# A decoder trunk for a prompt and eight samples: weight splits on VectorE, padded score rows, an earlier load, and output rows in two pieces

## The chip, the cores and the metric

The kernel runs on one core of a Trainium2 chip. The metric is the device time of one execution in microseconds (us); the time of a kernel is the median over its runs. Engines are named as the profile names them: PE is TensorE, DVE is VectorE, ACT is ScalarE, POOL is GpSimd, SP is SyncE, which issues most of the DMAs.

## The reference

The reference is one step of a two-layer decoder trunk. It runs for a prompt of 512 tokens and for eight samples of four new tokens each (32 in all), with the same weights and a width of 1024. In outline:

```python
def trunk(x, pos, pool_prev, ckv_past, krope_past, mem_k, mem_v, ...):
    # layer A
    z = rmsnorm(x, g_norm[0]) @ w_in_a[0]
    u, gate_t, q_m, gate_m = split(z)              # 1024, 1024, 512, 512
    tok = pool_mix(concat(prev, u), ...)           # trailing means of 2, 4, 8, 16, minus self, times w_pool_grp
    x = x + concat(tok * silu(gate_t), mem_attend(q_m) * silu(gate_m)) @ w_out[0]
    # the shared key/value side
    ckv, krope = shared_latent_kv(x, ...)          # 256 and 64 wide
    # layer B
    z = rmsnorm(x, g_norm[1]) @ w_in_b[0]
    c_q, gate_t, q_m, gate_m = split(z)            # 384, 1024, 512, 512
    tok = mla_mix(c_q, pos, concat(ckv_past, ckv), concat(krope_past, krope), ...)
    x = x + concat(tok * silu(gate_t), mem_attend(q_m) * silu(gate_m)) @ w_out[1]
    return rmsnorm(x, g_final), ...
```

In `mla_mix` eight heads attend over the latent: scores are `q_lat . ckv + q_rope . krope`, values are `p . ckv`, taken through `w_v_up` afterwards. The prompt attends to its own 512 positions. A sample attends to 4096 cached positions, which lie in 32 pages of 128 named by a page table, and to its own new rows. The outputs are the normalized streams of prompt and samples and the new states (pooling rows, latents, keys and values of the memory).

## The kernel before, in words

**Layout and precision.** Prompt and sample columns lie side by side, 544 columns, worked on in two halves of 272. Activations are transposed, so features are on the 128 partitions. Every large product is made of three matmuls: `split` (L88) casts an operand to its high part on ScalarE (L89) and subtracts it from the operand to get the low part (L90), on VectorE or on the engine that it is given; `mm3` (L93 to L96) then multiplies high by high (L94), high by low (L95) and low by high (L96) into one PSUM bank.

**Layer A.** The weights `w_in_a` come in slabs of 128 output features, a tile of 128x1024. `weights` (L234) loads a slab on SP into `wr` (three buffers) and splits it into `wh` and `wl` (two buffers each in the pool `pw`, and one more in `pw2`); without an engine given, GpSimd computes the low part. The memory attention comes first, then the pooling stage. In that stage ten slabs (the list `stage`: eight for the pooling branch's input, two for gates) are loaded and split ahead by `prepare_a` (L546), each two units before it is used. `pool_unit` (L571) makes one slab of the branch: the product, its evacuation by VectorE (L578, L581), then the running sums, also on VectorE: `g + 1` additions over 678 columns (L604), a correction of 16 columns (L606), the mean minus self for the prompt (L608) and for the samples (L611), and the split of the result. A gate's product is evacuated by VectorE too (L251, one per half), and its SiLU takes ScalarE and VectorE (L264, L265). `pool_mixed` multiplies two such slabs by a group's matrix and evacuates the product with the gate (L634). Four PSUM banks, `pa`, serve all these products, so TensorE goes on only when VectorE has emptied one.

**Layer B.** Behind the latent (`ckT_s` and `krT_s` keep its 32 new columns apart for the samples) stands a stage whose order is written by hand for PE and SP: generators yield estimates of their time, and `weave` (L956) always takes the one that is most behind. Their instructions stand in the program in that order. The threads are:

- the rounds over the samples' pages: `load_half` (L996) loads tiles `a` and `b` through SP; scores (L1051, L1062), transposes (L135), values (L1090)
- the prompt's heads
- `own_scores` (L1432), once: for each of eight samples, the scores of its 32 head-and-row queries against its four new rows, two matmuls over 128 rows of the latent (L1438) and one over the 64 rotary rows (L1441)
- `out_all`, the prompt's output projection: `out_rows(fh)` (L1379) for each half of the 1024 output columns. Six slabs of `w_out_b` (two 128-row blocks by 512 columns) are loaded into `wr` by `slab` (L1349) and split with GpSimd by `prepare`; for each slab the four row blocks of 128 tokens, in the order 0, 3, 1, 2, accumulate into four `oa` banks. `done` adds the residual (L1392) and squares and sums on ScalarE (L1393). For the second half it also adds the two halves' sums (L1398), takes the reciprocal root (L155 on VectorE, L159 on GpSimd), scales the first half on ScalarE (L1402) and the second half with the gain on VectorE (L1404), and stores both (L1403, L1405).
- `sample_out` (L1581), the samples' output: it issues the loads of five `w_out_b` slabs into `ws` (five buffers), then the load of `o`, the parts of all samples' attention that were stored in DRAM (`ostore`, L1585), then two tiles `vx` of `w_v_up` (L1590). `combine` joins the parts with the new rows' part (L1532), transposes, copies (L1549), and multiplies by `w_v_up` (L1561). Then twelve slabs are multiplied by 32 columns (L1598), a new slab's load going out as each buffer is read; the result is added to the residual (L1610), and behind both halves the samples are normalized (L1618).

VectorE, ScalarE and GpSimd are ordered by a scheduler that runs while the program is built, with estimates of its own. So an edit in one place can move instructions of these engines elsewhere.

Of the kernel before, what the change touches and what calls it, by code (L numbers as in the profile page):

```python
# [38 lines left out]
def trunk_kernel(ctx: ExitStack, tc: tile.TileContext, A, O):  # L39
# [506 lines left out]
    def prepare_a():  # L546
        if stage:
            f = stage.pop(0)
            ahead_a.append(weights(wa, f, pw2 if len(stage) % 3 == 1 else None))

# [236 lines left out]
    ckT_s = cst([P, 2, NS])  # L787
    krT_s = cst([64, NS])
    for f in range(2):
        nc.vector.tensor_copy(ckT_s[:, f, :], ck[f][:, SEQ:])  # L790
    nc.vector.tensor_copy(krT_s, kr[:64, SEQ:])
    ckx = [split(pc("c", F32R), pc("c", F32R), ck[f][:, :SEQ]) for f in range(2)]
# [546 lines left out]
    wo = A["w_out_b"]  # L1339
    ssq = st(8)  # L1340
    sss = st(2)
# [37 lines left out]
    def out_rows(fh):  # L1379
        pts = [ps_("oa") for _ in range(4)]  # L1380
        pts = [pts[j] for j in (0, 3, 1, 2)]

        def run(s, j, wh, wl):
            c = slice(j * P, (j + 1) * P)
            for i, k in enumerate(order[s]):
                h, l = mixed[k]
                mm3(pts[j], h[:, c], l[:, c], wh[:, i, :], wl[:, i, :], s == 0 and i == 0, s == 5 and i == 1)

        def done(j):
            f = slice(fh * 512, (fh + 1) * 512)  # L1390
            xf = x1n[j][:, f]
            nc.vector.tensor_tensor(out=xf, in0=pts[j], in1=xf, op=ALU.add)  # L1392
# [11 lines left out]
            nc.vector.scalar_tensor_tensor(out=xf, in0=xf, scalar=r, in1=gains_f[0][:, f], op0=ALU.mult, op1=ALU.mult)  # L1404
            nc.sync.dma_start(O["y_p"][0, j * P : (j + 1) * P, 512:], xf)  # L1405

        late = []
        for s in range(6):
# [4 lines left out]
            for j in range(4):  # L1413
                for one in late:
                    run(one[0], j, *one[1:])
                    yield 1.4, 0.0
                if s == 5:
                    if not x1n:
                        yield lambda: x1n
                    done(j)  # L1420
            for _ in late:
# [10 lines left out]
    def own_scores():  # L1432
# [3 lines left out]
        for b in range(NB):  # L1436
            for k in range(2):
# [3 lines left out]
            nc.tensor.matmul(  # L1441
                sv[:, b, :], lhsT=Qr[:64, b, 0, :], rhs=krT_s[:, b * NT : (b + 1) * NT], start=False, stop=True
            )
# [314 lines left out]
```

## Time and profile before

| | us |
|---|---|
| median of three runs | 838.99 |
| lowest and highest of them | 835.16, 840.82 |
| the profiled execution, its own time | 837.61 |
| its span in the profile | 835.8 |
| TensorE busy with matmuls | 793.3 |
| VectorE, ScalarE, GpSimd busy | 502.9, 326.7, 261.0 |

The page shows one execution. A row of a timeline has the start in us from the beginning of the span, the duration in us, the engine, the line, the operation, the tile written and the tile read, the shapes, and how many alike were merged (x4). In brackets stands how long the engine had been idle before it and what ended that idle time. A window's row gives busy time and count for each engine, then the granted TensorE clock (1.00 is full), the DMA share and GB/s. In the chain of waits each piece is released by the one before it, so its shares add up to the whole span. SPq is the queue of SP: the time it spends in issuing DMAs.

### The profile page before, as it was taken

What the parts mean: (1) busy time and instruction counts of PE and PEld (TensorE: products, weight loads), DVE (VectorE), ACT (ScalarE), POOL (GpSimd) and SP (SyncE); (2) the same over time, 40 slices, a digit from 0 to 9 for tenths busy, and PEclk for the clock granted to TensorE, in tenths of its full rate; (3) what the DMA queues carried; (4) which work ended last, traced back from release to release, by engine and by line L of the source; (5) the groups of instructions that cost most, each with busy time, mean ns of one, the idle gap of its engine ahead of it and who ended that gap; (6) DMA issues with size and microseconds to landing.
All of it is one profiled execution on the core that took longest, in us unless ns stands there. A gap on an engine that the chain in (4) does not pass through costs nothing.

```text
span 835.8 us, 17542 instructions
## 1 busy us (share of the span) xinstructions
PE 793.3 (95%) x6906; PEld 681.5 (82%) x6906; DVE 502.9 (60%) x941; ACT 326.7 (39%) x650; POOL 261.0 (31%) x213
## 2 busy tenths in 40 slices
PE   6999999988999999999999999899999999999995
PEld 6989998988999989877999897676767767767674
DVE  6757666797763435775766653665665577653313
ACT  7453343322243226335433423444443445342212
POOL 0035224444133313411522242642250230055321
PEclk9999999998999999999999999999999999999998
DMA  8355247421213234636624785967978767886652
GB/s 305 97 185 219 74 176 253 158 76 45 96 57 96 75 121 149 204 91 223 227 88 179 264 282 194 367 220 238 307 243 269 260 217 243 269 274 221 219 177 107
DMA packets 82101, 158.01 MB, mean 189 GB/s; under 512 B 9186, under 2 KB 34403, under 8 KB 81763
## 3 DMA queue, kind: packets, MB, share of 16 engines
q1 hardware_dynamic: 77170, 141.22, 50.7%
q0 software_dynamic: 4848, 15.67, 5.1%
q8 instruction: 54, 0.88, 0.4%
q14 instruction: 29, 0.23, 0.1%
HBM read 147.23 MB, written 9.64 MB: 188 GB/s over the span
## 4 chain that ended last, share of the span: by engine, by line
PE 72%; DVE 12%; DMA 8%; issue 2%; ACT 2%; POOL 2%; SPq 1%; POOLq 0%; DVEq 0%; ACTq 0%
PE pa L94 14%; PE pa L96 13%; PE pa L95 13%; PE tr L135 5%; PE ac L1051 3%; PE ac L1090 3%; DVE v L604 3%; DMA o<-ostore 2%; PE oa L94 2%; PE oa L95 2%; PE oa L96 2%; PE ac L1062 2%; PE ac L393 1%; DMA b<-in_cache_P 1%; DMA wr<-in_w_mem_v 1%
## 5 line engine op out<-in xcount | busy, mean ns | idle before, releaser
L94 PE MATMUL pa<-h,wh 128*128 128x272 f32 x832 | 240.2, 291 | 0.9 <-DVE g L634 0.9
L96 PE MATMUL pa<-h,wl 128*128 128x272 f32 x832 | 236.9, 290 | 0.7 <-POOL wl L90 0.7
L90 POOL TENSOR_TENSOR wl<-wr,wh 128x1024 fp32r<-128x1024 f32 (+1 forms) x67 | 154.8, 2311 | 232.3 <-ACT wh L89 220.9
L95 PE MATMUL pa<-h,wh 128*128 128x272 f32 x640 | 184.4, 289 | 0.0
L94 PEld LDWEIGHTS pa<-h,wh 128*128 128x128 f32 x832 | 157.1, 189 | 5.6 <-issue 3.5
L96 PEld LDWEIGHTS pa<-h,wl 128*128 128x128 f32 x832 | 155.7, 189 | 2.2 <-POOL wl L90 1.2
L89 ACT CAST wh<-wr 128x1024 fp32r<-128x1024 f32 (+1 forms) x87 | 87.7, 1008 | 173.2 <-PE pa L95 69.0
L95 PEld LDWEIGHTS pa<-h,wh 128*128 128x128 f32 x640 | 121.1, 189 | 1.0
L95 PE MATMUL pa<-g,wh 128*128 128x272 f32 x192 | 54.9, 289 | 0.5 <-DVE g L90 0.5
L265 DVE SCALAR_TENSOR_TENSOR g<-t,g 128x272 f32<-128x272 f32 x48 | 46.1, 968 | 13.9 <-ACT t L264 13.9
L264 ACT ACTIVATE t<-g 128x272 f32<-128x272 f32 x48 | 20.3, 429 | 82.2 <-DVE g L251 77.7
L135 PE MATMUL tr<-c,b 128*128 128x128 f32 x256 | 39.6, 277 | 3.0 <-DVE kt L1019 1.7
L94 PE MATMUL oa<-wh,c 128*128 128x512 f32 x96 | 39.5, 412 | 0.0
L95 PE MATMUL oa<-wl,c 128*128 128x512 f32 x96 | 38.0, 396 | 1.2 <-POOL wl L90 1.2
L135 PEld LDWEIGHTS tr<-c,b 128*128 128x128 f32 x256 | 29.6, 140 | 9.5 <-issue 3.0
L95 PEld LDWEIGHTS pa<-g,wh 128*128 128x128 f32 x192 | 36.2, 188 | 0.9 <-DVE g L90 0.9
L1017 ACT COPY kt<-tr 128x512 f32<-128x512 f32 x43 | 25.3, 589 | 26.3 <-PE tr L135 25.4
L1051 PE MATMUL ac<-kt,c 128*32 128x256 f32 x256 | 34.4, 386 | 0.0
L1051 PE MATMUL ac<-a,c 128*32 128x256 f32 x256 | 34.0, 386 | 0.0
L251 DVE SCALAR_TENSOR_TENSOR g<-pa,r 128x272 f32<-128x272 f32 x42 | 18.1, 437 | 25.8 <-PE pa L96 25.7
L90 DVE TENSOR_TENSOR q<-q,q 128x512 fp32r<-128x512 f32 x16 | 27.2, 1698 | 10.0 <-ACT q L89 9.9
L90 DVE TENSOR_TENSOR wl<-wr,wh 128x1024 fp32r<-128x1024 f32 x20 | 24.5, 1225 | 12.4 <-ACT wh L89 12.3
(380 smaller groups left out, 1813.9 us busy)
## 6 DMA issues: line engine op xcount, KB each, us to landing
a<-in_cache_P SPq DMA_DIRECT2D x128, 288.0 KB, 4.7
b<-in_cache_P SPq DMA_DIRECT2D x128, 160.0 KB, 4.9
wr<-in_w_in_a SPq DMA_DIRECT2D x24, 512.0 KB, 3.8
wr<-in_w_in_b SPq DMA_DIRECT2D x19, 512.0 KB, 3.6
cs<-in_mem_kT SPq DMA_DIRECT2D x16, 512.0 KB, 5.4
wr<-in_w_out_a SPq DMA_DIRECT2D x16, 384.0 KB, 3.1
wr<-in_w_out_b SPq DMA_DIRECT2D x12, 512.0 KB, 5.6
ws<-in_w_out_b SPq DMA_DIRECT2D x12, 512.0 KB, 5.5
```

The lines of the kernel that those rows point to most:

```text
L89: nc.scalar.copy(h, src)
L90: (eng or nc.vector).tensor_tensor(out=l, in0=src, in1=fr(h), op=ALU.subtract)
L94: nc.tensor.matmul(out, lhsT=wh, rhs=xh, start=start, stop=False)
L95: nc.tensor.matmul(out, lhsT=wh, rhs=xl, start=False, stop=False)
L96: nc.tensor.matmul(out, lhsT=wl, rhs=xh, start=False, stop=stop)
L135: nc.tensor.transpose(out, in_, ident[:k, :k])
L264: nc.scalar.activation(th[:, :HALF], z[:, o : o + HALF], AF.Tanh)
L265: nc.vector.scalar_tensor_tensor(out=z[:, o : o + HALF], in0=th[:, :HALF], scalar=1.0, in1=z[:, o : o + HALF], op0=ALU.add, op1=ALU.mult,)
L604: nc.vector.tensor_tensor(out=nx[:, lo:], in0=cur[:, lo:], in1=cur[:, lo - d : ULEN - d], op=ALU.add)
L1017: nc.scalar.copy(out, src)
L1051: nc.tensor.matmul(o[j * NS : (j + 1) * NS, :], lhsT=QT[:, k, b, :], rhs=(nat[ih][0][:, :, PGW + k * P : PGW + (k + 1) * P] if j < 2 else ...
L1090: nc.tensor.matmul(po[j * NS : (j + 1) * NS, :256], lhsT=pT[:, i * P + j * NS : i * P + (j + 1) * NS], rhs=nat[i // 2][j // 2][:, j % 2 * ...
```

## The change

The change has four parts.

1. `prepare_a` gives VectorE to `weights`, so the low parts of its ten slabs (L90, 128x1024) are computed by VectorE instead of GpSimd.
2. `krT_s` gets 128 rows instead of 64, set to zero by GpSimd beforehand, and the third matmul of each sample in `own_scores` runs over all 128 rows. The added rows of the query tile meet zeros.
3. In `sample_out` the loads of `o` and `vx` stand ahead of the five `ws` slabs' loads.
4. In `out_rows` the second half's last row block (tokens 256 to 383) becomes two pieces of 256 columns, the second one in an `ac` bank. Each piece has its own add and its own sum of squares. The squares are scaled as they are summed, so the mean needs no step of its own, and the sums are added up in steps before the last one is there (L1409, L1414 in the new numbering), then the root on GpSimd (L1417), then the scaling (L1418, L1421), still 512 columns wide.

```diff
@@ prepare_a
-            ahead_a.append(weights(wa, f, pw2 if len(stage) % 3 == 1 else None))
+            ahead_a.append(weights(wa, f, pw2 if len(stage) % 3 == 1 else None, nc.vector))
@@
-    krT_s = cst([64, NS])
+    krT_s = cst([P, NS])
+    nc.gpsimd.memset(krT_s, 0.0)
...
-    nc.vector.tensor_copy(krT_s, kr[:64, SEQ:])
+    nc.vector.tensor_copy(krT_s[:64], kr[:64, SEQ:])
@@
-    ssq = st(8)
+    ssq = st(16)
@@ out_rows
-        pts = [pts[j] for j in (0, 3, 1, 2)]
-
-        def run(s, j, wh, wl):
-            c = slice(j * P, (j + 1) * P)
+
+        pieces = [[(pts[j], 0, 512)] for j in (0, 3, 1, 2)]
+        if fh:
+            pieces[3] = [(pts[2], 0, 256), (ps_("ac"), 256, 256)]
+
+        def run(s, j, piece, wh, wl):
+            ps, o, n = piece
+            c, w = slice(j * P, (j + 1) * P), slice(o, o + n)
             for i, k in enumerate(order[s]):
                 h, l = mixed[k]
-                mm3(pts[j], h[:, c], l[:, c], wh[:, i, :], wl[:, i, :], s == 0 and i == 0, s == 5 and i == 1)
-
-        def done(j):
-            f = slice(fh * 512, (fh + 1) * 512)
+                mm3(ps[:, :n], h[:, c], l[:, c], wh[:, i, w], wl[:, i, w], s == 0 and i == 0, s == 5 and i == 1)
+
+        def done(j, p, ps, o, n):
+            f = slice(fh * 512 + o, fh * 512 + o + n)
             xf = x1n[j][:, f]
-            nc.vector.tensor_tensor(out=xf, in0=pts[j], in1=xf, op=ALU.add)
-            nc.scalar.activation(pat("wu"), xf, AF.Square, accum_out=ssq[:, 2 * j + fh : 2 * j + fh + 1])
+            nc.vector.tensor_tensor(out=xf, in0=ps[:, :n], in1=xf, op=ALU.add)
+            c = 4 * j + 2 * fh + p
+            nc.scalar.activation(pat("wu", n=n), xf, AF.Square, scale=D ** -0.5, accum_out=ssq[:, c : c + 1])
...
-            sq = st(1)
-            nc.vector.tensor_tensor(
-                out=sq, in0=ssq[:, 2 * j : 2 * j + 1], in1=ssq[:, 2 * j + 1 : 2 * j + 2], op=ALU.add
+            if p < len(pieces[j]) - 1:
+                return
+            sm = st(3)
+            others = [4 * j] + [4 * j + 2 + i for i in range(p)]
+            so_far = EPS
+            for i, o_ in enumerate(others):
+                nc.vector.tensor_scalar(
+                    out=sm[:, i : i + 1], in0=ssq[:, o_ : o_ + 1], scalar1=so_far, scalar2=None, op0=ALU.add
+                )
+                so_far = sm[:, i : i + 1]
+            r = st(1)
+            nc.vector.tensor_scalar(
+                out=sm[:, 2:3], in0=ssq[:, c : c + 1], scalar1=so_far, scalar2=None, op0=ALU.add
             )
-            r = rstd_cols(sq, 1, P, D)
+            nc.gpsimd.tensor_tensor(out=r, in0=sm[:, 2:3], in1=mhalf[:, :1], op=ALU.pow)
...
             for j in range(4):
-                for one in late:
-                    run(one[0], j, *one[1:])
-                    yield 1.4, 0.0
-                if s == 5:
...
-                    done(j)
+                for p, piece in enumerate(pieces[j]):
+                    for one in late:
+                        run(one[0], j, piece, *one[1:])
+                        yield 1.4 / len(pieces[j]), 0.0
+                    if s == 5:
...
+                        done(j, p, *piece)
@@ own_scores
-                sv[:, b, :], lhsT=Qr[:64, b, 0, :], rhs=krT_s[:, b * NT : (b + 1) * NT], start=False, stop=True
+                sv[:, b, :], lhsT=Qr[:, b, 0, :], rhs=krT_s[:, b * NT : (b + 1) * NT], start=False, stop=True
@@ sample_out
-        here = [slab(cb("ws"), *todo.pop(0)) for _ in range(5)]
         o = cb("o").rearrange("p (b c) -> p b c", b=NB - 1)
         nc.sync.dma_start(o, ostore.rearrange("b p c -> p b c"))
...
+        here = [slab(cb("ws"), *todo.pop(0)) for _ in range(5)]
```

The order of the instructions moves in three places that matter here. The first is VectorE in the pooling stage, around the evacuation of one gate: `g_2159` is that gate, `pa_2160` and `pa_2189` are the banks of its two halves, `v_` and `t_2152` are running sums and pooled rows. Before:

```order
L604 TENSOR_TENSOR v_2147<-v_2145 128x676
L251 SCALAR_TENSOR_TENSOR g_2159<-pa_2160,r_258 128x272
L604 TENSOR_TENSOR v_2149<-v_2147 128x672
L90 TENSOR_TENSOR g_2263<-g_362,h_2262 128x544
L606 TENSOR_TENSOR v_2149<-v_2149,c_79 128x16
L611 SCALAR_TENSOR_TENSOR t_2152<-v_2149,u_2079 128x32
L90 TENSOR_TENSOR g_2267<-g_371,h_2266 128x544
L608 SCALAR_TENSOR_TENSOR t_2152<-v_2149,u_2079 128x512
L265 SCALAR_TENSOR_TENSOR g_2159<-t_2186,g_2159 128x272
L90 TENSOR_TENSOR g_2465<-g_380,h_2464 128x544
L251 SCALAR_TENSOR_TENSOR g_2159<-pa_2189,r_258 128x272
L634 SCALAR_TENSOR_TENSOR g_763<-pa_2230,c_84,g_763 128x272
```

And with the change:

```order
L604 TENSOR_TENSOR v_2145<-u_2079 128x678
L90 TENSOR_TENSOR wl_2221<-wr_2218,wh_2220 128x1024
L90 TENSOR_TENSOR x_2076<-t_2072,x_2075 128x544
L604 TENSOR_TENSOR v_2147<-v_2145 128x676
L251 SCALAR_TENSOR_TENSOR g_2159<-pa_2160,r_258 128x272
L90 TENSOR_TENSOR g_2263<-g_362,h_2262 128x544
L604 TENSOR_TENSOR v_2149<-v_2147 128x672
L90 TENSOR_TENSOR g_2267<-g_371,h_2266 128x544
L251 SCALAR_TENSOR_TENSOR g_2159<-pa_2189,r_258 128x272
L606 TENSOR_TENSOR v_2149<-v_2149,c_79 128x16
L611 SCALAR_TENSOR_TENSOR t_2152<-v_2149,u_2079 128x32
L634 SCALAR_TENSOR_TENSOR g_763<-pa_2230,c_84,g_763 128x272
```

A slab's split stands in VectorE's queue now, and the evacuation of `pa_2189` has moved ahead of L606, L611, L608, L265 and the split of `g_2465`.

The second place is TensorE in the samples' output, where pairs of `ws` slabs alternate with the prompt's output rows (`oa_10106` and `oa_10109` are row blocks). Before:

```order
L1598 MATMUL ac_10198<-ws_9938,c_4176 32x128 x8
L1598 MATMUL ac_10198<-ws_9940,c_4176 32x128 x8
L94 MATMUL oa_10106<-wh_10102,c_9540 128x512
L95 MATMUL oa_10106<-wl_10103,c_9540 128x512
L96 MATMUL oa_10106<-wh_10102,g_9541 128x512
L94 MATMUL oa_10106<-wh_10102,c_9544 128x512
L95 MATMUL oa_10106<-wl_10103,c_9544 128x512
L96 MATMUL oa_10106<-wh_10102,g_9545 128x512
L1598 MATMUL ac_10198<-ws_9942,c_4176 32x128 x8
L1598 MATMUL ac_10198<-ws_10207,c_4176 32x128 x8
```

With the change (L1616 is the same matmul in the new numbering, `oa_10109` here the first piece of the last row block):

```order
L1616 MATMUL ac_10200<-ws_9945,c_4177 32x128 x8
L1616 MATMUL ac_10200<-ws_9947,c_4177 32x128 x8
L94 MATMUL oa_10109<-wh_10097,c_9527 128x256
L95 MATMUL oa_10109<-wl_10098,c_9527 128x256
L96 MATMUL oa_10109<-wh_10097,g_9528 128x256
L94 MATMUL oa_10109<-wh_10097,c_9531 128x256
L95 MATMUL oa_10109<-wl_10098,c_9531 128x256
L96 MATMUL oa_10109<-wh_10097,g_9532 128x256
L1616 MATMUL ac_10200<-ws_9949,c_4177 32x128 x8
L1616 MATMUL ac_10200<-ws_10209,c_4177 32x128 x8
```

Six matmuls of 256 columns stand between these pairs instead of six of 512, and behind the second pair the other piece, again six of 256, stands where six of 512 stood.

The third place is VectorE at the end of the program (`x_` are the row blocks, `s_` the sums and roots). Before:

```order
L1392 TENSOR_TENSOR x_9925<-oa_10108,x_9925 128x512
L1404 SCALAR_TENSOR_TENSOR x_9923<-x_9923,s_10464,g_9927 128x512
L1398 TENSOR_TENSOR s_10485<-s_9510 128x1
L155 TENSOR_SCALAR s_10487<-s_10485 128x1
L1404 SCALAR_TENSOR_TENSOR x_9925<-x_9925,s_10489,g_9927 128x512
```

With the change:

```order
L1397 TENSOR_TENSOR x_9926<-oa_10109,x_9926 128x256
L1414 TENSOR_SCALAR s_10484<-s_9511,s_10484 128x1
L1409 TENSOR_SCALAR s_10523<-s_9511 128x1
L1409 TENSOR_SCALAR s_10523<-s_9511,s_10523 128x1
L1421 SCALAR_TENSOR_TENSOR x_9924<-x_9924,s_10486,g_9928 128x512
L1397 TENSOR_TENSOR x_9926<-ac_10111,x_9926 128x256
L1414 TENSOR_SCALAR s_10523<-s_9511,s_10523 128x1
L1421 SCALAR_TENSOR_TENSOR x_9926<-x_9926,s_10526,g_9928 128x512
```

The last piece's add has moved behind the third block's scaling, and one VectorE step fewer stands between the last sum and the root.

More of the change, by code (lines that the diff above doesn't have):

```diff
@@ L1396, in done @@
                 return
-            sq = st(1)
-            nc.vector.tensor_tensor(
-                out=sq, in0=ssq[:, 2 * j : 2 * j + 1], in1=ssq[:, 2 * j + 1 : 2 * j + 2], op=ALU.add
+            if p < len(pieces[j]) - 1:
[11 more added lines that the diff above has]
+                out=sm[:, 2:3], in0=ssq[:, c : c + 1], scalar1=so_far, scalar2=None, op0=ALU.add
             )
-            r = rstd_cols(sq, 1, P, D)
+            nc.gpsimd.tensor_tensor(out=r, in0=sm[:, 2:3], in1=mhalf[:, :1], op=ALU.pow)
             nc.scalar.activation(x1n[j][:, :512], x1n[j][:, :512], AF.Copy, scale=r)
             nc.sync.dma_start(O["y_p"][0, j * P : (j + 1) * P, :512], x1n[j][:, :512])
-            nc.vector.scalar_tensor_tensor(out=xf, in0=xf, scalar=r, in1=gains_f[0][:, f], op0=ALU.mult, op1=ALU.mult)
+            xf = x1n[j][:, 512:]
+            nc.vector.scalar_tensor_tensor(out=xf, in0=xf, scalar=r, in1=gains_f[0][:, 512:], op0=ALU.mult, op1=ALU.mult)
             nc.sync.dma_start(O["y_p"][0, j * P : (j + 1) * P, 512:], xf)
@@ L1413, in out_rows @@
             for j in range(4):
-                for one in late:
-                    run(one[0], j, *one[1:])
-                    yield 1.4, 0.0
-                if s == 5:
-                    if not x1n:
-                        yield lambda: x1n
-                    done(j)
+                for p, piece in enumerate(pieces[j]):
[3 more added lines that the diff above has]
+                    if s == 5:
+                        if not x1n:
+                            yield lambda: x1n
+                        done(j, p, *piece)
             for _ in late:
```

## The prediction

> **What bounds the kernel now.** I read the page's busy shares first, then its chain of waits, then windows of busy time per engine around the four places that the change touches, and last the timeline rows there.
>
> ```profile
> PE 793.3 (95%) x6906; PEld 681.5 (82%) x6906; DVE 502.9 (60%) x941; ACT 326.7 (39%) x650; POOL 261.0 (31%) x213
> PE 72%; DVE 12%; DMA 8%; issue 2%; ACT 2%; POOL 2%; SPq 1%; POOLq 0%; DVEq 0%; ACTq 0%
> ```
>
> TensorE is busy for 793 of 835.8 us and is 72% of the chain that ended last. So an edit pays only where TensorE stands still, runs below its full clock, or runs matmuls that go away. The 42 idle us are spread over the program; the part that this change can reach shows in the windows of the pooling stage (columns: window, its length, busy time and count on PE, weight load, DVE, ACT, POOL, then granted clock, DMA share, GB/s):
>
> ```profile
> 174.00:180.00 6.00, 6.00 (x50) 6.00 (x49) 5.22 (x8) 0.93 (x2) 2.18 (x4) 1.00 0.34 102
> 180.00:186.00 6.00, 5.54 (x44) 5.29 (x42) 5.86 (x8) 1.86 (x5) 2.90 (x2) 1.00 0.30 76
> 186.00:192.00 6.00, 2.85 (x14) 2.67 (x13) 6.00 (x12) 2.27 (x4) 3.33 (x3) 0.65 0.00 1
> 192.00:198.00 6.00, 6.00 (x40) 6.00 (x40) 2.83 (x6) 0.00 (x0) 0.00 (x0) 0.78 0.20 66
> 204.00:210.00 6.00, 5.06 (x41) 4.84 (x40) 5.53 (x10) 2.41 (x5) 2.66 (x4) 1.00 0.39 125
> ```
>
> An undisturbed stretch holds 50 matmuls in 6 us, 0.12 us each. The next four miss 6, 36, 10 and 9: 61 matmuls, 61 x 0.12 = 7.3 us of TensorE's time lost here. VectorE is nearly full in the same stretches, and the granted clock falls to 0.65 and 0.78.
>
> **1. The ten low-part splits move from POOL to DVE.** TensorE's rows say whom it waits for: the evacuation of the gate's accumulator by VectorE (L251).
>
> ```profile
> 185.17 0.39 PE L94 MATMUL pa<-x,wh 128*128 128x272 f32 x1 [0.46 <-DVE g L251]
> 189.34 0.60 PE L94 MATMUL pa<-x,wh 128*128 128x272 f32 x1 [3.15 <-DVE g L251]
> ```
>
> VectorE reaches that evacuation late because single operations in its queue take far longer than their like:
>
> ```profile
> 154.69 2.77 DVE L90 TENSOR_TENSOR wl<-wg,wh 128x512 fp32r<-128x512 f32 x1
> ...
> 158.16 0.68 DVE L90 TENSOR_TENSOR wl<-wg,wh 128x512 fp32r<-128x512 f32 x1
> 159.11 1.73 DVE L604 TENSOR_TENSOR v<-v 128x672 f32<-128x672 f32 x2
> 161.18 1.95 DVE L606 TENSOR_TENSOR v<-v,c 128x16 f32<-128x16 f32 x1
> ...
> 166.28 3.81 DVE L604 TENSOR_TENSOR v<-v 128x672 f32<-128x672 f32 x2
> ...
> 173.56 2.52 DVE L604 TENSOR_TENSOR v<-u 128x678 f32<-128x678 f32 x1
> ...
> 180.99 2.87 DVE L604 TENSOR_TENSOR v<-u 128x678 f32<-128x678 f32 x1
> ...
> 186.44 0.17 DVE L606 TENSOR_TENSOR v<-v,c 128x16 f32<-128x16 f32 x1
> ...
> 188.85 0.43 DVE L251 SCALAR_TENSOR_TENSOR g<-pa,r 128x272 f32<-128x272 f32 x1
> ```
>
> Each slow row begins while GpSimd runs one of the splits and ends with it, or at most its own plain length later; for the row at 180.99 that is this one:
>
> ```profile
> 180.75 2.39 POOL L90 TENSOR_TENSOR wl<-wr,wh 128x1024 fp32r<-128x1024 f32 x1 [1.32 <-ACT wh L89]
> ```
>
> The excesses are 2.77 - 0.68 = 2.09, 1.95 - 0.17 = 1.78, 3.81 - 1.73 = 2.08, and 2.52 and 2.87 less a plain 0.87 (half of 1.73), 1.65 and 2.00: 9.6 us of VectorE's time in the five ahead of the evacuation at 188.85. The price of a split on VectorE itself stands in the group of the other w slabs, min/median/max in ns:
>
> ```profile
> L90 DVE TENSOR_TENSOR wl<-wr,wh x20: 1215/1226/1226, 17.7 to 390.3; 128x1024 fp32r<-128x1024 f32 x20
> ```
>
> Five of 1.23 are 6.1 us, so VectorE's queue up to that evacuation becomes 9.6 - 6.1 = 3.5 us shorter. Besides, the order of the change puts the evacuation of the second half (g_2159 from pa_2189) ahead of L606, L611, L608, L265 and one L90, which stood before it: from 186.44 to 188.85 are 2.41 us, less one L90 that stays ahead (0.68), 1.7. 188.85 becomes about 183.6. TensorE asks for that bank when the three matmul triples behind the 185.17 row are done, at 186.2, or 185.7 without that row's own 0.46 of wait. There are 2 us of slack: both waits go, and with them the half clock that follows the long one. At 207.8 the order also brings L634 forward past a running sum, and the wait of about 0.9 there goes too. I take the whole 7.3. From the other side: if the gaps close but the half clock stays, it is 7.3 - 2.4 (10 matmuls missing in 192:198, and 10 of the 36 in 186:192, since the gap of 3.15 is 26; 20 x 0.12) = 4.9; if each split adds its 1.23 and the excesses were something else, it is a loss (rival E). The order also brings two w_in_a loads ahead of loads for the running memory attention near 135 us, on SP; no row prices that, and I put +-0.5 on it, about the 0.46 above.
>
> The Trainium skill, TensorE: Matmul & The Clock Gate, in "HAM oscillation — how this bites in real kernels", asks for no TensorE idle gap above about 3.4 us to keep the clock. Here a gap of 3.15 us was followed by 0.65 and 0.78, so the measured row decides, and closing that gap is worth the clock's 2.4 us as well; by that bound of the Trainium skill the closing of the gap would owe the clock nothing, and the term would be 4.9.
>
> **2. Padded rows in the new rows' scores.** A matmul pair of 128 rows and the following one of 64 rows do not follow each other like two equal ones:
>
> ```profile
> 723.44 0.29 PE L1438 MATMUL tr<-c,c 128*32 128x4 f32 x4
> 723.66 0.22 PE L1441 MATMUL tr<-c,c 64*32 64x4 f32 x2
> ...
> 726.25 0.22 PE L1441 MATMUL tr<-c,c 64*32 64x4 f32 x2
> ```
>
> From 723.66 to 726.25 are seven periods of 0.37 us. The four passes of one L1438 group start within 0.08 us (0.29 long, 0.22 of it until the next begins), so six passes of one shape need about 0.19. 8 x (0.37 - 0.19) = 1.5 us less on TensorE, between zero and 8 x 0.37 = 3.0. What hides it is the next wait: w_out_b's slab, whose load waits in SP's own queue, and its split.
>
> ```profile
> 728.24 2.46 SPq L1008 DMA_DIRECT2D b<-in_cache_P  x4
> 730.79 1.60 SPq L1349 DMA_DIRECT2D wr<-in_w_out_b  x3
> ```
>
> ```profile
> 737.13 1.05 ACT L89 CAST wh<-wr 128x1024 fp32r<-128x1024 f32 x1 [1.41 <-DMA wr<-in_w_out_b]
> ```
>
> ```profile
> 740.74 0.51 PE L95 MATMUL oa<-wl,c 128*128 128x512 f32 x1 [1.25 <-POOL wl L90]
> ```
>
> SP issues without a pause up to 730.79, then load, cast and split run one behind the other. The edit moves none of these, so TensorE reaches 740.74 earlier and waits 2.7 instead of 1.25. I take 0. If that cover were gone it would be -1.5; if the longer wait cost the clock as the 3.15 did (half speed for some 3.4 us, rival C), +1.7.
>
> **3. The samples' parts first.** TensorE waits for them once:
>
> ```profile
> 765.43 15.73 DMA o<-ostore
> ```
>
> ```profile
> 781.21 0.64 PE L1532 MATMUL tr<-o,t 128*32 128x256 f32 x8 [1.21 <-DMA o<-ostore]
> ```
>
> The load is issued behind five slabs of 512 KB and lands behind them. Ahead of them it lands earlier by more than the 1.21, which goes. The slabs land later instead, but are read only after the whole combine of the parts. SP's order moves nothing else there. Two matmul groups later TensorE needs VectorE's copy at 788.42:
>
> ```profile
> 788.42 0.87 DVE L1549 COPY t<-tr 128x128 f32<-128x128 f32 x4
> ```
>
> It sits behind four L1395 on VectorE, and the new order has one 512-column group less in front of its reader, which then waits about 0.35.
>
> **4. The last block in two pieces.** Its 36 matmuls of 512 columns become 72 of 256, at these starts:
>
> ```profile
> 587.22 0.28 PE L95 MATMUL pa<-wul,c 128*128 128x256 f32 x1
> 587.34 0.28 PE L96 MATMUL pa<-wuh,c 128*128 128x256 f32 x1
> ```
>
> ```profile
> 826.60 0.40 PE L95 MATMUL oa<-wl,c 128*128 128x512 f32 x1
> 826.83 0.40 PE L96 MATMUL oa<-wh,g 128*128 128x512 f32 x1
> ```
>
> 2 x 0.12 against 0.23: at most 0.01 x 36, I take +0.2. The pieces change where the sample output is woven in: between slab pairs now stand six matmuls of 256 columns instead of 512, twice. The eighth slab's load is issued when the third slab's buffer is free, and TensorE already waits for it:
>
> ```profile
> 798.61 5.41 DMA ws<-in_w_out_b
> ```
>
> ```profile
> 804.06 0.64 PE L1598 MATMUL ac<-ws,c 128*32 128x128 f32 x16 [0.32 <-DMA ws<-in_w_out_b]
> ```
>
> It is asked for 2 x 6 x 0.12 = 1.4 us sooner after its release, so this wait grows by about 1.4, and with the pieces' own refill by up to 1.5. From below the cost is nothing, if the load lands sooner than 5.41 since other traffic fell away. I take +1.5, since 5.41 is its own row. The end is the chain behind the last matmul:
>
> ```profile
> 827.26 0.69 DVE L1392 TENSOR_TENSOR x<-oa,x 128x512 f32<-128x512 f32 x1 [0.89 <-PE oa L96]
> ...
> 829.82 0.75 DVE L1404 SCALAR_TENSOR_TENSOR x<-x,s,g 128x512 f32<-128x512 f32 x1 [0.66 <-POOL s L159]
> ```
>
> The last piece's add and Square cover 256 columns (about 0.3 + 0.25 less) and one VectorE step goes (0.2), but in VectorE's order the third block's L1421 of 0.75 stands ahead of the last add and TensorE finishes the piece while it runs, which gives about 0.5 back, and the last scaling is 512 wide as before. I take -0.05, between -0.8 and +0.3.
>
> **The sum**, against the profiled execution's own 837.6: -7.3 + 0 - 1.2 + 0.35 + 0.2 + 1.5 - 0.05 = -6.5, 831.1. The runs shown have their median 1.4 higher, from which it would be 832.5. I say 831.8.
>
> **Rivals.**
> B, the tail costs nothing: the slab lands in time and the copy is there, and the end gains its 0.8. For it: 0.32 is a small wait. Against: the shorter distance stands in the order. -7.3 - 1.2 + 0.2 - 0.8 = -9.1: about 829.2.
> C, the longer wait at 740 halves the clock: +1.7, about 833.5. For it: 3.15 did so at 186. Against: a 1.73 us gap at 671 (the transposes' wait for L1019) did not; its row is
>
> ```profile
> 671.38 0.65 PE L135 MATMUL tr<-c,b 128*128 128x128 f32 x4 [1.73 <-DVE kt L1019]
> ```
>
> and 2.7 lies between the two, nearer to 3.15.
> D, the stall in the pooling stage only moves: VectorE still comes late, to another bank or to the split slab that TensorE now gets from the same queue. For it: VectorE is full from 180 to 192. Only the 9 matmuls of 204:210 come back: 837.6 + 0.8 - 1.1 = 837.3.
> E, slower: VectorE's queue is in order, so a split that stands ahead of its cast makes all behind it wait for ScalarE. GpSimd's splits waited for their casts (1.32 in the row at 180.75). If that is so for six of the ten, at 1.9 us each (that 1.32 and half a cast of 1.05), the queue is 6 x 1.9 - 3.5 = 7.9 longer and TensorE waits that long for its banks: 845.5. It decides from 0.6 us per split on (3.5 / 6). Against: walking the new order with these durations, the casts end 0.3 to 1.4 us before VectorE gets to their splits.
>
> **How the numbers follow.** Chances: forecast 0.50, B 0.18, C 0.13, D 0.12, E 0.07. One per cent, 8.4 us, is about what a measurement tells from no change; faster by more means under 830.6. The forecast's own spread is 829 to 834.5 and a good third of it lies there (0.18); with B that is 0.36. Slower by over 1% means over 847.4, E's dearer part, 0.05. The rest is 0.59. The range 828 to 837 leaves out E, D's upper half and B's lowest part.
>
> **What would show it.** Right: between 180 and 198 us no TensorE gap above 0.5 and a granted clock of 1.00; 128x1024 splits on DVE near 1.23 and running sums near 0.87; six passes of the new scores in about 0.19; the wait at 740 longer and at the same time after SP's issue; no wait for o; a wait of 1.5 to 2 for a ws slab about 30 us before the end. Wrong: a wait of TensorE for a split on VectorE in the pooling stage (D or E), a granted clock below 0.9 right behind 740 (C), or an end that is more than 0.5 us shorter from the last matmul on (B).

## The result and the profile after

The median of 17 runs is 833.63 us (829.82 to 839.41), beside 838.63 us for the kernel before (17 runs). The ratio is 0.9936 with a 95% interval of 0.9913 to 0.9959, some 5 us less. The forecast was 831.8, with 828 to 837 as its range. The sum was near, but the term for the padding was wrong, and that for the earlier `o` load probably too small, as the profile and the experiments show.

The profiled execution of the changed kernel took 836.59 us, 3 more than the median, so its rows show where things happen, and the medians say what they are worth. First the windows of the pooling stage, in the columns of before:

```profile
174.00:180.00 6.00, 6.00 (x50) 6.00 (x49) 5.29 (x11) 1.90 (x4) 0.37 (x3) 1.00 0.39 102
180.00:186.00 6.00, 6.00 (x50) 6.00 (x49) 6.00 (x13) 1.70 (x3) 0.50 (x1) 1.00 0.27 77
186.00:192.00 6.00, 6.00 (x50) 6.00 (x49) 5.73 (x11) 1.27 (x2) 0.51 (x2) 1.00 0.24 67
192.00:198.00 6.00, 6.00 (x50) 6.00 (x49) 4.44 (x9) 1.91 (x4) 0.87 (x3) 1.00 0.25 70
```

TensorE runs 50 matmuls in each stretch at the full clock. In the first two VectorE does 11 and 13 operations where it did 8. Its queue around the evacuation of the gate's second half:

```profile
178.46 0.87 DVE L604 TENSOR_TENSOR v<-u 128x678 f32<-128x678 f32 x1
179.25 1.22 DVE L90 TENSOR_TENSOR wl<-wr,wh 128x1024 fp32r<-128x1024 f32 x1
...
184.18 0.43 DVE L251 SCALAR_TENSOR_TENSOR g<-pa,r 128x272 f32<-128x272 f32 x1
```

Every row has its plain length, the split costs 1.22, and the evacuation that came at 188.85 comes at 184.18 (183.6 was forecast). The gain can be read at the next wait for the same thing, in before and after:

```profile
225.82 0.40 PE L94 MATMUL pa<-x,wh 128*128 128x272 f32 x1 [0.37 <-DVE g L634]
```

```profile
218.68 0.39 PE L94 MATMUL pa<-x,wh 128*128 128x272 f32 x1 [0.37 <-DVE g L634]
```

225.82 - 218.68 = 7.14 us, where 7.3 stood in the sum. The new rows' scores, first and last pair:

```profile
720.22 0.29 PE L1456 MATMUL tr<-c,c 128*32 128x4 f32 x4
720.36 0.20 PE L1459 MATMUL tr<-c,c 128*32 128x4 f32 x2
...
721.57 0.27 PE L1456 MATMUL tr<-c,c 128*32 128x4 f32 x4
```

The period is (721.57 - 720.22) / 7 = 0.19 instead of 0.37, as forecast. What became of these 1.5 us stands in the rows and windows that follow:

```profile
732.70 0.33 PE L135 MATMUL tr<-c,b 128*128 128x128 f32 x1 [0.43 <-DMA b<-in_cache_P]
...
735.33 0.47 PE L100 MATMUL po<-p,vx 128*128 128x128 f32 x1 [1.51 <-ACT p L89]
...
737.66 0.79 PE L95 MATMUL oa<-wl,c 128*128 128x512 f32 x1 [0.89 <-POOL wl L90]
```

```profile
732.00:736.00 4.00, 2.06 (x14) 1.59 (x13) 0.69 (x2) 1.79 (x3) 0.75 (x1) 0.90 0.64 240
736.00:740.00 4.00, 3.11 (x9) 2.12 (x9) 4.00 (x3) 1.89 (x3) 4.00 (x2) 0.50 0.70 254
740.00:744.00 4.00, 4.00 (x15) 3.20 (x14) 1.54 (x2) 0.00 (x0) 3.64 (x4) 0.75 0.84 256
```

One wait of 1.25 us has become three, 2.8 together, ahead of the output projection. The clock is at half behind them: a granted 0.90, 0.50 and 0.75 in stretches of 4 us are 0.8 + 4 + 2 = 6.8 us at half speed. TensorE's lead over before, which is 740.74 - 737.66 = 3.1 at the split slab, is 1.1 ten us later, at the next scores of the samples:

```profile
750.50 0.41 PE L1051 MATMUL ac<-a,c 128*32 128x256 f32 x2
```

```profile
749.36 0.41 PE L1052 MATMUL ac<-a,c 128*32 128x256 f32 x2
```

In the tail the wait for `o` is gone, so the same multiplication starts 781.21 - 778.78 = 2.4 earlier than before:

```profile
778.78 0.64 PE L1550 MATMUL tr<-o,t 128*32 128x256 f32 x8
```

The wait for the eighth `ws` slab has grown from 0.32 to 1.74, where 0.32 + 1.4 was forecast:

```profile
800.31 0.64 PE L1616 MATMUL ac<-ws,c 128*32 128x128 f32 x16 [1.74 <-DMA ws<-in_w_out_b]
```

And the end, VectorE after the third block's scaling:

```profile
826.21 0.75 DVE L1421 SCALAR_TENSOR_TENSOR x<-x,s,g 128x512 f32<-128x512 f32 x1
826.87 0.42 DVE L1397 TENSOR_TENSOR x<-ac,x 128x256 f32<-128x256 f32 x1
...
828.80 0.75 DVE L1421 SCALAR_TENSOR_TENSOR x<-x,s,g 128x512 f32<-128x512 f32 x1 [0.66 <-POOL s L1417]
```

The last matmul ends at 826.38 here and 827.23 before; the last scaling starts 2.42 and 2.59 behind it. So the end gains 0.17: the third block's scaling does stand in the way of the last add.

In between, this execution also lost time at two places that the change doesn't touch: a wait for a GpSimd split, 1.68 instead of 0.50 near 340, and a wait for a page's DMA near 631, with a granted clock of 0.60 behind it.

```profile
631.38 0.33 PE L135 MATMUL tr<-c,b 128*128 128x128 f32 x1 [1.96 <-DMA b<-in_cache_P]
```

```profile
632.00:636.00 4.00, 4.00 (x30) 3.21 (x32) 2.19 (x6) 1.45 (x5) 0.00 (x0) 0.60 0.51 185
```

TensorE's wait for the page load near 631 was 0.26 to 1.27 us in six of the other seven kernels with the same splits, and 2.10, again with a half clock behind it, in the seventh (parts 1 to 3 with six more splits on VectorE); in the five kernels without these splits it was 0.6 at most. So a TensorE that comes earlier can give some of its lead back here. How much differs from profile to profile, and in this execution it is part of why it lies 3 us above its median.

### The profile page after: what moved, and what is told of

It reads as the page before. It is cut to its first block, busy times and chain, and to the rows that moved or that the text cites. A ratio compares the mean times of both kernels' runs of the same rounds, so it can differ in the third digit from the quotient of the medians.

```text
span 834.8 us, 17623 instructions
## 1 busy us (share of the span) xinstructions
PE 792.2 (95%) x6942; PEld 682.7 (82%) x6942; DVE 497.2 (60%) x953; ACT 326.4 (39%) x652; POOL 235.5 (28%) x204
## 4 chain that ended last, share of the span: by engine, by line
PE 81%; DVE 7%; DMA 6%; ACT 2%; issue 1%; POOL 1%; SPq 0%; POOLq 0%; DVEq 0%; ACTq 0%
PE pa L94 16%; PE pa L96 15%; PE pa L95 15%; PE tr L135 6%; PE ac L1052 4%; PE ac L1091 3%; PE oa L94 3%; PE oa L95 3%; PE oa L96 3%; PE ac L1063 2%; PE ac L393 1%; DMA wr<-in_w_mem_v 1%; PE hs L135 1%; POOL wl L90 1%; DMA c<-in_c_cos 1%
## 5 line engine op out<-in xcount | busy, mean ns | idle before, releaser
L96 PE MATMUL pa<-h,wl 128*128 128x272 f32 x832 | 236.1, 289 | 1.9 <-POOL wl L90 1.9
L90 POOL TENSOR_TENSOR wl<-wr,wh 128x1024 fp32r<-128x1024 f32 (+1 forms) x57 | 129.2, 2267 | 209.4 <-ACT wh L89 206.2
L95 PE MATMUL pa<-h,wh 128*128 128x272 f32 x640 | 183.6, 288 | 0.0
L96 PEld LDWEIGHTS pa<-h,wl 128*128 128x128 f32 x832 | 154.9, 188 | 3.4 <-POOL wl L90 2.3
L265 DVE SCALAR_TENSOR_TENSOR g<-t,g 128x272 f32<-128x272 f32 x48 | 42.9, 902 | 13.0 <-ACT t L264 13.0
L90 DVE TENSOR_TENSOR wl<-wr,wh 128x1024 fp32r<-128x1024 f32 x30 | 36.7, 1223 | 14.8 <-ACT wh L89 14.7
L94 PE MATMUL oa<-wh,c 128*128 128x512 f32 (+1 forms) x96 | 38.9, 406 | 0.0
L95 PE MATMUL oa<-wl,c 128*128 128x512 f32 (+1 forms) x96 | 37.5, 391 | 0.9 <-POOL wl L90 0.9
L90 DVE TENSOR_TENSOR q<-q,q 128x512 fp32r<-128x512 f32 x16 | 27.2, 1699 | 10.0 <-ACT q L89 9.9
```

The lines of the kernel that those rows point to most:

```text
L90: (eng or nc.vector).tensor_tensor(out=l, in0=src, in1=fr(h), op=ALU.subtract)
L94: nc.tensor.matmul(out, lhsT=wh, rhs=xh, start=start, stop=False)
L95: nc.tensor.matmul(out, lhsT=wh, rhs=xl, start=False, stop=False)
L96: nc.tensor.matmul(out, lhsT=wl, rhs=xh, start=False, stop=stop)
L265: nc.vector.scalar_tensor_tensor(out=z[:, o : o + HALF], in0=th[:, :HALF], scalar=1.0, in1=z[:, o : o + HALF], op0=ALU.add, op1=ALU.mult,)
```

## The experiments

Theory: the splits win about 7 us in the pooling stage and keep them; the earlier `o` load wins about 1; the padded scores win nothing, since a wait follows them, and can cost the clock; the two pieces cost 1.5. Rival: the parts of the tail win something together, and the splits are worth less than 7. The first four kernels do one part each.

**Part 1 alone**

```diff
-            ahead_a.append(weights(wa, f, pw2 if len(stage) % 3 == 1 else None))
+            ahead_a.append(weights(wa, f, pw2 if len(stage) % 3 == 1 else None, nc.vector))
```

> The kernel before with VectorE's splits alone (part 1). Theory: the stall in the pooling stage goes as in the whole change, no TensorE gap above 0.5 us and a granted clock of 1.00 from 174 to 216 us, and the span there is 7 us shorter; nothing in the tail differs from before (TensorE waits 1.2 for the o load, 0.3 for a ws slab). Time: 7 us under before, ratio about 0.9915, and at or below that of the whole change. Rival: the gain needs the other parts too, or part of it is given back at later DMA waits; then the ratio is 0.995 or more.

Measured: 832.65 us, ratio 0.9931 (0.9905 to 0.9958), 6.1 under the 838.72 of before in its runs. TensorE's waits of 0.46, 3.15 and 0.94 are gone, and nothing else of the change was needed. 6.1 is less than 7.1, though the interval, 3.5 to 8.0 us, holds both. The profile is of the slowest of its six executions (837.50), and it shows a place where lead is given back, the tail:

```profile
776.40 1.08 PE L1532 MATMUL tr<-o,t 128*32 128x256 f32 x8 [2.22 <-DMA o<-ostore]
```

```profile
774.00:778.00 4.00, 1.78 (x17) 0.40 (x16) 0.00 (x0) 0.77 (x3) 2.33 (x1) 0.78 0.95 319
778.00:782.00 4.00, 4.00 (x28) 1.67 (x21) 1.43 (x3) 0.87 (x2) 2.35 (x1) 0.50 0.35 125
782.00:786.00 4.00, 4.00 (x12) 3.02 (x11) 2.27 (x4) 0.67 (x2) 0.00 (x0) 0.50 0.40 131
786.00:790.00 4.00, 4.00 (x40) 3.20 (x42) 0.89 (x4) 0.46 (x1) 0.00 (x0) 0.94 0.01 2
```

TensorE arrives 5.8 us earlier than in before (at 774.18 instead of 780.00), but the `o` load lands only 4.8 earlier (at 776.36 instead of 781.16), so the wait grows from 1.21 to 2.22; behind it the clock is at half for 1.8 + 4 + 4 + 0.5 = 10.2 us.

**Part 2 alone**

```diff
-    krT_s = cst([64, NS])
+    krT_s = cst([P, NS])
+    nc.gpsimd.memset(krT_s, 0.0)
...
-    nc.vector.tensor_copy(krT_s, kr[:64, SEQ:])
+    nc.vector.tensor_copy(krT_s[:64], kr[:64, SEQ:])
...
-                sv[:, b, :], lhsT=Qr[:64, b, 0, :], rhs=krT_s[:, b * NT : (b + 1) * NT], start=False, stop=True
+                sv[:, b, :], lhsT=Qr[:, b, 0, :], rhs=krT_s[:, b * NT : (b + 1) * NT], start=False, stop=True
```

> The kernel before with the padded score rows alone (part 2). Theory: TensorE is 1.5 us quicker through the new rows' scores, and the half clock that follows them in before (727 to 730.5 us) goes too, but the wait for the split slab near 740 takes all of it: no change, ratio 1.000, if the clock stays up behind the longer waits. Rival (the clock): the longer waits near 732 to 740 halve the clock for about 3.4 us behind the first matmul of the output projection, where nothing hides it: 1.7 us slower, ratio 1.002. Second rival: the gain of 1.5 to 3 us arrives, ratio 0.998 or less.

Measured: 840.22 us, ratio 1.0025 (1.0006 to 1.0045): slower by 1.5 at the median. Its rows and windows show the rival's way:

```profile
736.86 0.33 PE L100 MATMUL po<-p,vx 128*128 128x128 f32 x1 [2.45 <-ACT p L89]
...
739.19 0.80 PE L95 MATMUL oa<-wl,c 128*128 128x512 f32 x1 [1.39 <-POOL wl L90]
```

```profile
736.00:740.00 4.00, 1.75 (x6) 1.32 (x7) 3.16 (x4) 3.28 (x5) 3.22 (x2) 0.90 0.49 173
740.00:744.00 4.00, 4.00 (x13) 3.17 (x13) 3.05 (x2) 0.00 (x0) 3.64 (x4) 0.67 0.86 305
```

Two waits, 3.84 us together with four short matmuls between them, and then 0.8 + 2.6 = 3.4 us at half clock in the output projection, which has nothing to hide it: half of that time is lost, 1.7 us.

**Part 3 alone**

```diff
-        here = [slab(cb("ws"), *todo.pop(0)) for _ in range(5)]
         o = cb("o").rearrange("p (b c) -> p b c", b=NB - 1)
...
             nc.sync.dma_start(v[k], src)
+        here = [slab(cb("ws"), *todo.pop(0)) for _ in range(5)]
```

> The kernel before with the samples' parts fetched ahead of the five slabs (part 3). Theory: the wait of 1.2 us for the o load at 780 goes and the wait for VectorE's copy near 789 takes back 0.3 at most: 1 us less, ratio 0.999; the wait for the ws slab near 804 stays at 0.3, since the distance between the slabs is as before. Rival: the slabs, now behind the o load, come late themselves, and the sum is zero or a loss.

Measured: 835.92 us, ratio 0.9971 (0.9949 to 0.9993): 2.8 less at the median (0.6 to 4.3 by the interval), where 1 was expected. The row that waited 1.21 now follows its predecessor without a wait, the next one in the chain waits 0.45 (0.35 was worked out), and the wait for the `ws` slab is still 0.32.

```profile
788.33 1.08 PE L1561 MATMUL tr<-vx,t 128*32 128x128 f32 x32 [0.45 <-PE oa L96]
```

The row names TensorE's own L96, but the copy that it reads (L1549 on VectorE) ran from 787.55 to 788.42, so that copy is what it waited for. These rows give 1.2 - 0.45 = 0.8 only, which the interval still holds. If there is more, it may be the clock behind the wait for `o`, which the profiles of parts 1 and 2 alone show at half and that of before doesn't; this is not shown, since the profiles are one execution each.

**Part 4 alone**

```diff
+        pieces = [[(pts[j], 0, 512)] for j in (0, 3, 1, 2)]
+        if fh:
+            pieces[3] = [(pts[2], 0, 256), (ps_("ac"), 256, 256)]
```

with what belongs to it in `run`, `done` and the loop.

> The kernel before with the last row block in two pieces and the sums in steps (part 4). Theory: TensorE's wait for a ws slab between the first and second half of the samples' output grows from 0.3 to 1.7 us, the end behind the last matmul is only 0.1 to 0.2 shorter: 1.3 to 1.5 us slower, ratio 1.0016. Rival: the end gains the 0.8 that two pieces could give, and the sum is between a gain of 0.5 and a loss of 0.5.

Measured: 840.74 us, ratio 1.0032 (1.0008 to 1.0056), 2.0 slower. The wait has the expected length, and here the clock drops behind it too (0.75 and 0.82 in stretches of 4 us, 3.4 us at half):

```profile
801.20 0.64 PE L1615 MATMUL ac<-ws,c 128*32 128x128 f32 x16 [1.67 <-DMA ws<-in_w_out_b]
```

```profile
800.00:804.00 4.00, 2.80 (x22) 2.00 (x22) 0.00 (x0) 0.08 (x1) 2.35 (x1) 0.75 1.03 372
804.00:808.00 4.00, 4.00 (x60) 2.74 (x62) 0.00 (x0) 0.00 (x0) 0.00 (x0) 0.82 0.24 88
```

Alone the parts are worth -6.1, +1.5, -2.8 and +2.0 at their medians, together -5.4; the whole change measured -5.0.

**Parts 1 and 3**

The two diffs above, on the kernel before.

> Parts 1 and 3 together on the kernel before, without the padding and the pieces. Theory: the parts that win add up. With the splits alone TensorE waited 2.22 us for the o load and 0.5 for a ws slab (it comes to both earlier, the loads do not), so the earlier o load is worth up to 2.2 here: ratio near 0.990, about 830.5, and under the whole change by 3 us. Rival: the padding or the pieces do something useful in the whole change; then this is no faster than it.

Measured: 829.38 us, ratio 0.9895 (0.9867 to 0.9924). By the medians the `o` load is worth 832.65 - 829.38 = 3.3 behind the splits, though the intervals of the two still overlap. Unlike what the expectation says, the `o` load does come earlier behind the splits, only by less than TensorE does. With half of its edits the change gains 9 us instead of 5.

**The whole change with one piece**

```diff
-        if fh:
+        if False:
             pieces[3] = [(pts[2], 0, 256), (ps_("ac"), 256, 256)]
```

> The whole change with the last row block in one piece again (parts 1 to 3; the sums stay in steps). Theory: the wait for the ws slab shrinks from 1.7 to about 0.3 us and 0.2 of overhead goes, the end grows by 0.2: 1.5 us under the whole change, ratio about 0.992. Against the run of parts 1 and 3 it shows the price of the padding, 0 to 2 us. Rival: no difference from the whole change, so the cost of the pieces seen alone was noise.

Measured: 830.40 us, ratio 0.9893 (0.9866 to 0.9920). It is 3.2 under the whole change; the wait for the slab is 0.54. Beside parts 1 and 3 its median is 1.0 higher, but the ratios do not tell the two apart, so this pair alone doesn't settle the padding's price.

**The whole change, pieces paired**

```diff
             for j in range(4):
+                if s < 5:
+                    for one in late:
+                        for piece in pieces[j]:
+                            run(one[0], j, piece, *one[1:])
+                        yield 1.4, 0.0
+                    continue
                 for p, piece in enumerate(pieces[j]):
```

> The whole change, but both pieces of a slab run one behind the other in the first five slabs, so that as much work of TensorE stands between the pairs of ws slabs as in before. Theory (the distance between the slab pairs makes the wait): the wait for the eighth ws slab falls from 1.74 to about 0.3 and the time to 1.4 us under the whole change, ratio about 0.992. Rival (the slab comes late for other reasons, such as the o load ahead of the slabs): the wait stays above 1 us, the time as in the whole change.

Measured: 831.52 us, ratio 0.9919 (0.9887 to 0.9950), 2.1 under the whole change at the median; the intervals overlap, so the row says more than the time. The multiplication that waited 1.74 follows without a wait of its own, with the `o` load still ahead of the slabs: its pair of slabs is one row, 0.36 longer than the 1.08 of the pairs before it.

```profile
795.48 1.44 PE L1622 MATMUL ac<-ws,c 128*32 128x128 f32 x32
```

So the distance between the slab pairs makes the wait, not the order of the loads.

**GpSimd's splits twice, on the kernel before**

```diff
-            ahead_a.append(weights(wa, f, pw2 if len(stage) % 3 == 1 else None))
+            t, v = load_w(wa[f], KD, P)
+            wh, wl = split_w(t, KD, P, nc.gpsimd, pw2 if len(stage) % 3 == 1 else None)
+            nc.gpsimd.tensor_tensor(out=wl, in0=t.rearrange("p (k c) -> p k c", k=KD), in1=fr(wh), op=ALU.subtract)
+            ahead_a.append((wh, wl))
```

> The kernel before, with each of the ten low parts computed twice by GpSimd (the second writes the same values over the first). It tells whether GpSimd's splits are what makes VectorE's operations long. Theory: VectorE's excess in the pooling stage about doubles, from 16 to some 30 us between 132 and 205 us (single running sums of 2.5 to 5 instead of 0.87), and TensorE's waits for VectorE there grow by 5 us or more: ratio above 1.006. Rival (VectorE's operations are long for reasons of their own, such as waits that the profile counts as busy): the excess and the time stay, except where TensorE waits for the longer split itself.

Measured: 855.11 us, ratio 1.0188 (1.0151 to 1.0226), 16 us more. VectorE's groups in this stage, first of before, then with the doubled splits (where L604 is L607):

```profile
L604 DVE TENSOR_TENSOR v<-v 128x676 f32<-128x676 f32 x6 | 7.2, 1204 | 0.1
...
L90 DVE TENSOR_TENSOR wl<-wg,wh 128x512 fp32r<-128x512 f32 x4 | 4.8, 1203 | 0.0
```

```profile
L607 DVE TENSOR_TENSOR v<-v 128x676 f32<-128x676 f32 x6 | 11.4, 1905 | 0.1
...
L90 DVE TENSOR_TENSOR wl<-wg,wh 128x512 fp32r<-128x512 f32 x3 | 8.9, 2977 | 0.0
```

The excess over the plain 0.85 and 0.68 goes from 0.35 to 1.05 and from 0.52 to 2.30 an operation; over all such groups of that stage (each mean less its plain length, times the count) it goes from some 17 to over 30 us. TensorE's wait for the gate's evacuation, 3.15 in before, is now 5.12:

```profile
198.00 0.60 PE L94 MATMUL pa<-x,wh 128*128 128x272 f32 x1 [5.12 <-DVE g L251]
```

That VectorE is slowed by what GpSimd does beside it is thereby shown.

**Parts 1 and 3, with six more low parts on VectorE**

```diff
-        wh, wl = split(fin("wh", F32R), fin("wl", F32R), t, nc.gpsimd)
+        wh, wl = split(fin("wh", F32R), fin("wl", F32R), t, nc.vector if fh == 0 else nc.gpsimd)
```

> Parts 1 and 3, and the low parts of the six slabs of the output projection's first half on VectorE instead of GpSimd. Theory (what ends the wait near 735 us is GpSimd's split of 2.4, which VectorE does in 1.2): TensorE's wait of 1.40 for the split slab falls to 0.3 or less, and VectorE's own operations beside it lose their excess (4.85 us for two splits of 128x512 becomes 1.4): 1.2 us under parts 1 and 3, ratio about 0.988. Rival: the DMA brings the next slabs no earlier, or the pieces of work queued on VectorE hold the split back; no change from parts 1 and 3.

Measured: 827.49 us, ratio 0.9855 (0.9826 to 0.9885), the fastest of all, 1.9 under parts 1 and 3 at the median, though the intervals overlap. The split takes 1.23, the wait for it, which was 1.40, has gone, and one of 0.61 for another operation of VectorE, now queued behind the split, has taken its place:

```profile
732.35 0.33 PE L102 MATMUL po<-p,vx 128*128 128x128 f32 x1 [0.61 <-DVE p L90]
732.51 0.45 PE L94 MATMUL oa<-wh,c 128*128 128x512 f32 x1
732.79 0.39 PE L95 MATMUL oa<-wl,c 128*128 128x512 f32 x1
```

**The same with the padding**

The edit of the run before, on the whole change with one piece (parts 1 to 3).

> Parts 1, 2 and 3 (with the padding) and the same six low parts on VectorE. Theory: with the split quicker, the two waits behind the padded scores are shorter; if they stay under the sum that halved the clock in the runs with the padding (2.4 and 1.7 us waits, then 0.5 to 0.6 of the clock), the padding is worth up to 1.5 us: at or under the kernel with parts 1 and 3 and the six low parts. Rival: the load still sets the end of the wait, the clock is halved behind it, and it is 0 to 2 us slower than that kernel.

Measured: 830.04 us, ratio 0.9896 (0.9864 to 0.9927), 2.5 over the kernel without the padding on the same chip. The waits there are 1.21 and 0.86. The time is on the rival's side (0 to 2 slower), but this execution's clock didn't drop behind them, so its one profile doesn't show where its runs lose the 2.5.

**The whole change without the padding**

The edit of part 2 taken back, on the whole change.

> The whole change without the padded rows (parts 1, 3 and 4). Theory: the padding saves TensorE's time only in front of a wait and can cost the clock behind it, so without it the time is the same or up to 1.7 us less than the whole change: ratio 0.991 to 0.994. Rival: the padding is worth its 1.5 us, and this is 1 us or more slower than the whole change, ratio 0.995 or more.

Measured: 831.02 us, ratio 0.9903 (0.9871 to 0.9935), 2.6 under the whole change. In four pairs (alone, parts 1 and 3, the same with six low parts, the whole change) the padded kernel's median is 1.5, 1.0, 2.5 and 2.6 higher. The third pair is the clearest (826.13 to 828.89 us without, 828.70 to 832.47 with the padding); the second has no difference in its ratios (0.9895 and 0.9893). So the padding won time in none of the four and cost some in most.

## Why the prediction was right, and where its steps failed

**Part 1** held by mechanism and size: -7.3 forecast, -7.1 in the profile, -6.1 in the median of the part alone. The reason was right too (the doubled splits), and the evacuation came 0.6 us from the forecast time. No run takes the shorter queue and the new order apart; by the forecast's own terms the queue's 3.5 us alone would have brought the evacuation to 185.4, ahead of the 186.2 at which TensorE asks, and the order's 1.7 alone only to 187.2. (From the row at 185.17 on TensorE runs two triples until 186.2, not three; the time stands.) What the sum left out is that a load which comes earlier by less than TensorE does makes a longer wait: 1 us more at the `o` load in the profile of part 1 alone, and up to 1.5 more at the page load near 631. The forecast priced part 3 at the wait in before.

**Part 2** is the step that failed: "I take 0". The work was right (1.5 us less on TensorE) and so was the wait behind it, which rose from 1.25 to 2.8 and in the part alone to 3.84. Rival C, with 0.13, is the one that the runs bear out: +1.7 forecast, +1.0 to +2.6 between the medians of four pairs. Its price was taken from the wait of 3.15, but the windows there, 0.65 and 0.78 in 6 us each, are 4.2 + 2.6 = 6.8 us at half clock; behind the padding's waits it was 3.4 in two profiles and 6.8 in two. The step also overlooked that the clock already fell in before, at the same scores, ahead of the wait:

```profile
722.80:726.40 3.60, 3.60 (x54) 3.06 (x52) 1.59 (x3) 0.78 (x2) 0.55 (x1) 1.00 0.93 318
726.40:728.40 2.00, 2.00 (x34) 1.19 (x32) 1.05 (x6) 0.23 (x1) 0.00 (x0) 0.69 1.04 353
```

That stretch at half clock stands ahead of the wait at 740, which could hide it. With the padding it is gone, TensorE arrives earlier by that too and waits longer, and the half clock comes behind the wait, where it costs its 1.7. A halved clock right behind the scores stands in six of the eight profiles without the padding (before among them) and in none of the five with it; behind the waits it stands in four of the five with it and in none of the eight. In these four the waits ahead of the output projection add up to 2.75 to 3.84 us, in the other nine profiles to 2.07 at most. So the half clock goes with long waits there, but each profile is one execution, and the kernel with the padding and six more splits on VectorE is 2.5 slower though its profile has no half clock there. That the half clock is the whole price of the padding is therefore likely, not shown. The Trainium skill (TensorE: Matmul & The Clock Gate, "Part 1: The HAM clock gate (the "warmup" mystery)") states windows of 3.4 us that run freely and a half clock after an idle one. The lengths agree, since the windows of the profiles gave 3.4, 6.8 and 10.2 us at half clock, one, two or three times 3.4. An idle gap of a full window wasn't needed here: 1.67 and 2.22 us did it, and 1.74 in the profile of the whole change and 1.87 in that without the padding didn't. Where in such a window each gap fell, no run shows.

**Part 3** was forecast at -1.2 + 0.35 and measured -2.8 alone and -3.3 behind the splits. The row-by-row estimate was right (the wait gone, 0.45 in its place). In the whole change the second wait doesn't appear. The size was probably too small, though the 0.85 lies inside the interval of part 3 alone (0.6 to 4.3): the wait was priced at the length that it has in before, and without a clock that can fall behind it.

**Part 4** was forecast at 0.2 + 1.5 - 0.05 = +1.65, and measured +2.0 alone (0.7 to 4.7 by the interval), and 3.2 as the step from one piece to the whole change. The wait (1.74) and the end (0.17 shorter) came as worked out; the paired pieces took the wait away again, and 2.1 us at the median. That the end gains little because another block's scaling stands ahead was right.

The total, -6.5, lies near the measured -5.0 because the terms' errors against the parts alone (+1.2 for part 1, +1.5 for part 2, -2.0 for part 3, +0.4 for part 4) nearly cancel, which is luck. Of the four only that of part 2 is outside the noise. Rivals B, D and E fell: the tail did cost, the stall did not move, and VectorE's splits did not wait long for their casts. The last column of their group in the changed kernel, from 130 to 210 us, is the idle time before them, 2.5 us for all ten:

```profile
L90 DVE TENSOR_TENSOR wl<-wr,wh 128x1024 fp32r<-128x1024 f32 x10 | 12.2, 1221 | 2.5 <-ACT wh L89 2.5
```

## What to carry to other kernels

Before moving work to an idle engine or away from it, look whether single operations of the busy engine become two or three times as long while the other runs: those rows give the price of the neighbour, and moving work onto the full engine can shorten its queue. Work saved ahead of a wait whose end it doesn't move was worth nothing here, and probably cost the clock behind the wait; look for what ends the wait and shorten that (here the split of 2.4 us that VectorE does in 1.2). Price each edit of a bundle alone: two of four edits here gave back 4 us of the 9 that the other two won.

## What the runs showed of the hardware

- GpSimd's subtraction of 128x1024 took 2.36 to 3.06 us and stretched single operations that VectorE ran beside it by 1.1 to 2.1 us; the same subtraction on VectorE took 1.22. It was cheaper for VectorE to do the work than to run beside it.
- Six passes of 4 columns over 128 rows followed one another in 0.19 us; with two of the six over 64 rows the period was 0.37. Filling up the rows halved the time of the scores.
- Waits of TensorE of 1.7 to 2.5 us, and pairs of shorter ones with a few short matmuls between, were followed by 3.4, 6.8 or 10.2 us at half clock in some profiles and by none in others.
